# Softmax sums applied after the value product: one division for two heads, the sums spread by DMAs through DRAM

## The chip, the cores and the metric

The kernel runs on one core of a Trainium2 chip. The metric is the device time of one launch in microseconds (us). The time before is the median of three runs; next to it stands one profiled execution, from which every duration below is taken.

## The reference, cut to what matters

The program is a small decoder trunk on one sequence of 512 tokens with 1024 channels: one state-space layer with its MLP, a shared projection for keys, values and forget gates, one layer of forgetting attention with its MLP, and a final norm. All of it is float32. The change lies in the attention alone, 16 heads of 64 channels:

```python
def one_block(args):                       # one block of 128 queries
    s = jnp.einsum('bhqd,bhkd->bhqk', qb, k)
    s = s + fq[..., None] - cum_log_f[:, :, None, :]
    s = jnp.where(mask[None, None], s, -jnp.inf)
    p = jax.nn.softmax(s, axis=-1)         # exp(s - max) / sum
    return jnp.einsum('bhqk,bhkd->bhqd', p, v)
```

Dividing each row of exponentials by its sum before the product with v, or dividing the row of the product by that sum afterwards, gives the same result.

## The kernel before, in words

Matrix products are made from float32 values split into a high and a low part (float32r), with three passes per product; ScalarE (ACT) copies the high part out and VectorE (DVE) subtracts to get the low part. Large weights come in 512 KB loads `st` (line 113), are split by ACT (line 124) into `wt`, and the low part of these splits is made in the attention by GpSimd (POOL, line 128).

The attention is a list of 64 steps, `steps`: head 0 to 15, and in each head four query blocks `i` of 128 rows; block `i` sees `i+1` blocks of 128 keys. It is a schedule written out by hand (`manual_schedule`, line 1411): each engine, and SyncE's queue of DMAs (SP), issues its instructions in the order in which the loop over `n` emits them. In one turn of this loop the letters of `CFG["seq"]` are called in order, `s f o q l a n t p x` for even `n` and `s o f l n t a p x q` for odd `n`:

- `s` makes the logits of step n on TensorE (PE) (`st_s`, lines 1210 to 1212, into `psx`), the row maximum on DVE and the exponential on ACT with the row sum accumulated beside it (`st_x`, lines 1218 and 1220). Where `i` is 3 it also issues five DMAs on SP that bring the next but one head's keys and queries (`st_h`, line 1203).
- `n` divides the exponentials of step n: a reciprocal of 128x1 and a multiplication of 128 rows by 128 to 512 columns on DVE (`st_n`, lines 1225 and 1229).
- `t` transposes the exponentials of step n-1 on PE (`st_t`, line 1234, into `ptp`), `p` copies them out as high and low part (`st_p`, ACT line 1249, DVE line 1250).
- `a`, at odd `n`, multiplies two blocks with the values (`st_av`, line 1268, into `po`). The left operand holds the values' high and low part side by side, so that `po` has 128 partitions for one head.
- `q` and `o` take a finished head out (`st_o`): ACT copies the lower half of `po` into `of` (line 1275), one turn later DVE adds the upper half (line 1277). Two heads share one `of` of 128x512; after the second head ACT copies it to `ot` (line 1281), and a turn later DVE makes the low part (line 1283).
- `f` puts one piece of other matrix work on PE into the turn: the key and value projections of later heads (lines 810 and 1130), later the first half of the output projection (`pw`, line 810). At every fourth turn such a piece opens a new weight chunk, and then ACT splits the next `st`. `l` runs deferred work: POOL's low part, and behind it on SP the next load `st`, which waits for POOL; and DVE's additions (line 1334) and low parts.

So DVE, ACT and SP each have one order, and a wait of one instruction holds all that stand behind it there. Instructions written after the loop (the preparation of the next MLP's first weights from `sr`, lines 887 to 899) are placed in between by the program's planner. Temporary tiles `tmp` rotate over four buffers.

After the loop the last head is taken out, and the second half of the output projection (`po`, line 810) and the next MLP follow.

Of the kernel before, what the change touches and what calls it, by code (L numbers as in the profile page):

```python
# [9 lines left out]
F32 = mybir.dt.float32  # L10
F32R = mybir.dt.float32r
I32 = mybir.dt.int32
AF = mybir.ActivationFunctionType
ALU = mybir.AluOpType
AX = mybir.AxisListType
PSUM = bass.MemoryType.PSUM

P = 128
SEQ = 512
# [10 lines left out]
NH = 16  # L30
HD = 64
EPS = 1e-6
MAGIC = 12582912.0
TWO_PI = 2.0 * math.pi
CFG = dict(seq=['sfoqlantpx', 'soflntapxq'], pat=[2, 1, 1, 1, 1, 1, 1, 1, 1, 1, 1, 1, 1, 1, 1, 1, 1, 1, 1, 1, 1, 1, 1, 1, 1, 1, 1, 1, 1, 1, 1, 1, 1, 1, 0, 2, 1, 1, 1, 1, 1, 1, 1, 1, 1, 1, 1, 1, 1, 1, 1, 1, 1, 1, 1, 1, 1, 1, 1, 1, 1, 1, 2, 1, 1, 1], nl=4, nt=1, u0=66, ns=[], wk=4, st=['f u02 u03 u10 u11 u12 s u13 c0 c1', 't t u02 f t u03 u10 u11 t u12 u13 s c0 c1'], x='GGGGGGGGGGVbb', m0=3)
WQ = "AABBABABAB"
ORDER = """
LR mR kz gnl win2V_0 win1V_0 decS_0 dl_1 rxv wina_0 gl_1 sw_2_0 gn win2V_1 xsS_1_1 dl_0 gR sw_2_1 xsS_0_1 tk
# [19 lines left out]
def body(tc, x, mix_norm, mlp_norm, mlp_w1, mlp_w2, log_dt, a_re, a_im, b_re, b_im,  # L58
         c_re, c_im, ssm_d, w_glu, kv_norm, w_kvf, b_f, wq, wo, final_norm, out):
    nc = tc.nc  # L60
    V, S, G, TE, DMA = nc.vector, nc.scalar, nc.gpsimd, nc.tensor, nc.sync

    with ExitStack() as ctx:
# [14 lines left out]
        def act_t(name):  # L78
            return ap_.tile([P, 2, SEQ], F32R, name=name, tag="act")

        def pst(name):
            return ps.tile([P, 512], F32, name=name, tag="ps")

        ident = cp.tile([P, P], F32, name="ident")
# [666 lines left out]
        hp = ctx.enter_context(tc.tile_pool(name="hp", bufs=1))  # L751
        m2 = ctx.enter_context(tc.tile_pool(name="m2", bufs=2))
        kvp = ctx.enter_context(tc.tile_pool(name="kvp", bufs=1))

        def act2_t(name):
            return m2.tile([P, 2, SEQ], F32R, name=name, tag="act2", bufs=8)

        def tmp_t(name, bufs=4):
            return m2.tile([P, SEQ], F32, name=name, tag="tmp", bufs=bufs)
# [235 lines left out]
        for mp in range(KT // 2):  # L995
            if mp == CFG["m0"]:
                u0 = Mix(mlp_w1_[0], 0, H, arena)
                run(u0.prep())
            for n in (2 * mp, 2 * mp + 1):
                c0 = n % 2 * D + n // 2 * 256  # L1000
# [77 lines left out]
        for m in range(KT):  # L1078
            h = act_t("hq")
# [6 lines left out]
        for k0 in (0, 3, 6):  # L1086
            nk_ = min(3, KT - k0)
            st = stp.tile([P, 4, 256], F32, name="st", tag="st").rearrange("p k n -> p (k n)")[:, 0:nk_ * VF]
            st = st.rearrange("p (k n) -> p k n", n=VF)
# [115 lines left out]
        def st_s(hd, i):  # L1205
            X = HX[hd % 2]
            n = P * (i + 1)
            qs = slice(i * P, (i + 1) * P)
            psx = pst("psx")
            TE.matmul(psx[:, 0:n], QT[hd // 2][:, hd % 2, qs], X[:, 0, 0:n], start=True, stop=False)  # L1210
            TE.matmul(psx[:, 0:n], X[0:66, 1, qs], X[0:66, 2, 0:n], start=False, stop=False)
            TE.matmul(psx[:, i * P:n], identr, mneg_r, start=False, stop=True)
            return psx

        def st_x(psx, i):
            n = P * (i + 1)
            mx = m2.tile([P, 3], F32, name="mx", tag="mx", bufs=6)
            V.tensor_reduce(mx[:, 0:1], psx[:, 0:n], AX.X, ALU.max, negate=True)  # L1218
            pb_ = m2.tile([P, SEQ], F32, name="prob", tag="prob", bufs=2)
            S.activation(pb_[:, 0:n], psx[:, 0:n], AF.Exp, bias=mx[:, 0:1], accum_out=mx[:, 1:2])  # L1220
            return pb_, mx

        def st_n(pb_, mx, i):
            n = P * (i + 1)
            V.reciprocal(mx[:, 2:3], mx[:, 1:2])
            if i in CFG["ns"]:
                S.activation(pb_[:, 0:n], pb_[:, 0:n], AF.Copy, scale=mx[:, 2:3])
            else:
                V.tensor_scalar(pb_[:, 0:n], pb_[:, 0:n], mx[:, 2:3], None, ALU.mult)  # L1229

        def st_t(pb_, i):
            ptp = pst("ptp")
            for kt in range(i + 1):
                TE.transpose(ptp[:, kt * P:(kt + 1) * P], pb_[:, kt * P:(kt + 1) * P], ident)  # L1234
            return ptp
# [36 lines left out]
        def st_o(hd):  # L1272
            po, of = head["po"], head["of"]
            rs = slice((hd % 2) * 64, (hd % 2) * 64 + 64)
            S.activation(of[rs], po[64:128], AF.Copy)
            yield
            V.tensor_tensor(of[rs], po[0:64], of[rs], op=ALU.add)
            if hd % 2:
                ot = act_t("ot")
                OT.append(ot)  # L1280
                S.activation(ot[:, 0], of, AF.Copy)
                yield
                V.tensor_tensor(ot[:, 1], of, ot[:, 0].bitcast(F32), op=ALU.subtract)
# [53 lines left out]
        NST = len(steps)  # L1337
# [15 lines left out]
        def at_s(n):  # L1353
            if n == CFG["u0"]:
                u0.arena = make_arena()
            if CFG["u0"] <= 60 and n in (CFG["u0"], 60):
                later.extend([lambda: next(u0p, 0)] * (8 if n < 60 else 3))
            if n < NST:
                ex[n] = st_x(st_s(*steps[n]), steps[n][1])
                hd, i = steps[n]  # L1360
                if i == 3 and hd + 2 < NH:
                    st_h(hd + 2)
# [19 lines left out]

        def at_t(n):
            if 0 <= n - 1 < NST:
                tp[0] = st_t(ex[n - 1][0], steps[n - 1][1])

        def at_n(n):
            if n < NST:
                st_n(*ex[n], steps[n][1])

        def at_p(n):
            if 0 <= n - 1 < NST:
# [176 lines left out]
```

## Time and profile before

| | |
|---|---|
| median of 3 runs | 1200.35 us (1198.94 to 1211.31) |
| profiled execution, its own time | 1199.35 us |
| span of this execution, first to last instruction | 1197.6 us |
| PE matmul busy | 1119.2 us, 93% of the span |
| DVE busy | 912.1 us, 76% |
| ACT busy | 607.8 us, 51% |
| POOL busy | 291.2 us, 24% |
| mean granted TensorE clock | 0.972 of full speed |

The profile lists for each engine how long it was busy; a group of instructions is named by line, engine, operation and tile. Idle time stands with the work that ended it ("releaser"). The time outside the span is 1.75 us. The attention's 64 steps run from about 636 to 813 us.

### The profile page before, as it was taken

How to read it: one execution, taken by the hardware profiler on the slowest of the kernel's cores; microseconds unless marked ns; L12 is line 12 of the kernel's file. 1: busy time of each engine (PE TensorE's matmuls, PEld its weight loads, DVE VectorE, ACT ScalarE, POOL GpSimd, SP SyncE). 2: the span in 40 equal slices, each digit the busy share in tenths (PEclk: the TensorE clock that was granted, in tenths of full speed). 3: DMA queues.
4: the chain of work that ended last, by engine and by line, in shares of the span. 5: the costliest groups of instructions: out<-in, count | busy, mean ns of one | idle time of the engine just before them, and what ended most of it. 6: DMA issues, size and time to landing. Idle time of an engine off the chain costs nothing.

```text
span 1197.6 us, 19030 instructions
## 1 busy us (share of the span) xinstructions
PE 1119.2 (93%) x7189; PEld 996.8 (83%) x7189; DVE 912.1 (76%) x1639; ACT 607.8 (51%) x1106; POOL 291.2 (24%) x298
## 2 busy tenths in 40 slices
PE   1678899999999999999999999888899999999997
PEld 1567688899999898998888999776899898999986
DVE  8976548799877778768566878875999777778754
ACT  4985355454434444336345666554755444343433
POOL 4234214422121212203102222314322312213101
PEclk9878899999999999999999999989899999999999
DMA  7997753143322323233244444311143323233222
GB/s 165 218 183 151 176 165 106 42 143 99 122 90 90 107 86 124 88 103 117 65 132 133 107 107 133 98 54 53 35 128 104 111 82 124 88 117 96 89 88 71
DMA packets 109388, 131.37 MB, mean 110 GB/s; under 512 B 9360, under 2 KB 87984, under 8 KB 109296
## 3 DMA queue, kind: packets, MB, share of 16 engines
q1 hardware_dynamic: 104432, 117.57, 32.9%
q0 software_dynamic: 4864, 12.59, 6.1%
q8 instruction: 57, 0.93, 0.3%
q14 instruction: 35, 0.29, 0.1%
HBM read 103.21 MB, written 2.74 MB: 88 GB/s over the span
## 4 chain that ended last, share of the span: by engine, by line
PE 79%; DVE 8%; DMA 5%; ACT 3%; issue 3%; SPq 0%; POOL 0%; DVEq 0%; ACTq 0%; POOLq 0%
PE pu L919 25%; PE po L810 16%; PE pvs L1484 14%; PE pk L810 6%; PE pv L810 6%; PE pvs L1130 2%; PE po L1268 2%; DMA cc<-dt 1%; PE ptp L1234 1%; PE pf L1118 1%; DMA TW<-tB 1%; DVE prob L1229 1%; DMA bc<-in_ssm_b_im_dram 1%; DMA TW<-kd 1%; PE pv L731 1%
## 5 line engine op out<-in xcount | busy, mean ns | idle before, releaser
L919 PE MATMUL pu<-hm,ar 128*128 128x256 f32 x1536 | 228.9, 284 | 3.2 <-ACT hm L863 2.2
L919 PEld LDWEIGHTS pu<-hm,ar 128*128 128x128 f32 x1536 | 204.4, 193 | 4.5 <-ACT hm L863 2.6
L810 PE MATMUL po<-at,wt 128*128 128x512 f32 x768 | 176.9, 389 | 0.0
L1484 PE MATMUL pvs<-wt,at 128*128 128x512 f32 (+1 forms) x768 | 175.5, 388 | 0.0
L898 POOL TENSOR_TENSOR ar<-ar,st 128x256 f32<-128x256 f32 x62 | 71.8, 1160 | 423.1 <-DVE ar L894 404.3
L124 ACT ACTIVATE wt<-st 128x1024 fp32r<-128x1024 f32 x110 | 116.2, 1057 | 114.0 <-PE po L810 30.3
L810 PEld LDWEIGHTS po<-at,wt 128*128 128x128 f32 x768 | 143.2, 188 | 29.1
L1484 PEld LDWEIGHTS pvs<-wt,at 128*128 128x128 f32 x768 | 142.6, 188 | 28.8
L128 DVE TENSOR_TENSOR wt<-st,wt 128x1024 fp32r<-128x1024 f32 x90 | 117.1, 1302 | 27.9 <-ACT wt L124 27.7
L919 PE MATMUL pu<-hd,x 128*128 128x256 f32 x768 | 136.3, 285 | 0.0
L887 ACT ACTIVATE ar<-ar 128x512 fp32r<-128x512 f32 x128 | 77.0, 627 | 89.9 <-PE pu L919 83.7
L919 PEld LDWEIGHTS pu<-hd,x 128*128 128x128 f32 x768 | 113.4, 193 | 2.9 <-issue 0.5
L888 DVE TENSOR_TENSOR ar<-ar 128x512 fp32r<-128x512 f32 x128 | 88.8, 700 | 31.0 <-ACT ar L887 31.0
L887 ACT ACTIVATE x<-st 128x512 fp32r<-128x512 f32 x62 | 36.3, 625 | 99.8 <-PE pvs L1484 48.9
L128 POOL TENSOR_TENSOR wt<-st,wt 128x1024 fp32r<-128x1024 f32 x20 | 48.2, 2408 | 143.6 <-ACT wt L124 125.5
L894 DVE TENSOR_TENSOR ar<-st 128x512 f32<-128x512 f32 x62 | 50.6, 819 | 32.8 <-DMA st<-in_mlp_w_dram 32.1
L810 PE MATMUL pv<-zt,wt 128*128 128x512 f32 x312 | 72.4, 391 | 0.2 <-ACT hT L992 0.2
L810 PEld LDWEIGHTS pv<-zt,wt 128*128 128x128 f32 x312 | 58.2, 188 | 12.3 <-ACT hT L992 0.4
L1220 ACT ACTIVATE prob<-psx,mx 128x128 f32<-128x128 f32 (+1 forms) x64 | 33.8, 528 | 60.2 <-DVE mx L1218 60.2
L899 POOL TENSOR_TENSOR ar<-ar,st 128x256 f32<-128x256 f32 x62 | 60.4, 977 | 4.2
L1039 ACT ACTIVATE at<-c 128x512 fp32r<-128x512 f32 x64 | 39.7, 630 | 39.3 <-DVE c L1037 39.1
L1025 DVE TENSOR_TENSOR hT<-hT,po 128x512 f32<-128x512 f32 x64 | 43.4, 679 | 16.8 <-PE po L810 16.8
(333 smaller groups left out, 2046.2 us busy)
## 6 DMA issues: line engine op xcount, KB each, us to landing
st<-in_mlp_w_dram SPq DMA_DIRECT2D x126, 512.0 KB
st<-in_ssm_w_glu_dram SPq DMA_DIRECT2D x16, 512.0 KB
st<-in_w_kvf_dram SPq DMA_DIRECT2D x14, 512.0 KB
hx<-kt SPq DMA_DIRECT2D x48, 128.0 KB
Win<-tB POOLq DMA_DIRECT2D x8, 512.0 KB, 7.3
TW<-tB POOLq DMA_DIRECT2D x8, 512.0 KB, 6.3
TW<-kd SPq DMA_DIRECT2D x8, 512.0 KB
st<-in_attn_wq_dram SPq DMA_DIRECT2D x8, 512.0 KB
```

The source lines that it names most:

```text
L124: S.activation(wt[:, 0], st, AF.Copy)
L128: (G if slot[1] == "A" and CFG["x"][7 + lows[0] % 3] == "G" else V).tensor_tensor(wt[:, 1], st, wt[:, 0].bitcast(F32), op=ALU.subtract)
L810: TE.matmul(pts[m], wt[:, a, k, m * P:(m + 1) * P], acts[k0 + k][:, b], start=(first and k0 == parts[0][0] and k == 0 and n == 0), stop=(k ...
L887: S.activation(X[0], src, AF.Copy)
L888: V.tensor_tensor(X[1], src, X[0].bitcast(F32), op=ALU.subtract)
L894: V.tensor_tensor(Ta[:, :, js].rearrange("p w j n -> p j w n"), f[:, :, 1:3], f[:, :, 0:1].broadcast_to([P, 2, 2, P]), op=ALU.add)
L898: e.tensor_tensor(Tb[:, 0, js], Ta[:, 0, js], v[:, :, 1, 0], op=ALU.add)
L899: e.tensor_tensor(Tb[:, 1, js], Tb[:, 0, js], v[:, :, 1, 1], op=ALU.add)
L919: TE.matmul(self.acc[p], self.W[p][:, a, j], self.H.moving(p, j, b), start=(p == g[0] and j == 0 and n == 0), stop=(p == g[-1] and j == 3 ...
L1025: V.tensor_tensor(hT[:, m, :], hT[:, m, :], po[j], op=ALU.add)
L1039: S.activation(at_[:, 0], c, AF.Square)
L1484: TE.matmul(po[:, cols], A[k][:, b], wts[k // 2][:, a, k % 2, cols], start=start and n == 0, stop=stop and n == 3 * len(ks) - 1)
```

## The change

The exponentials are no longer multiplied by the reciprocal of their sum. The sums of two heads go into one tile `sums` of 128x8 (a column for each head and block). One turn after the pair's last step (`n`, `st_r`) DVE takes the reciprocal of all eight columns, and SP writes them to DRAM transposed, as 8 rows of 128. One turn later (`st_d`) SP reads them back in two DMAs, each with one head's row of 512 repeated over 64 partitions, into `rb` (128x512). When the pair is taken out, `of` is multiplied by `rb` on DVE, one turn after the addition; the copy to `ot` and its low part follow after that. The last pair does without DRAM: eight small matmuls with the reciprocals as left operand and the identity as right operand spread them into a tile of PSUM, and the multiplication follows the addition directly.

```diff
+        dq = ctx.enter_context(tc.tile_pool(name="dq", bufs=1, space=bass.MemoryType.DRAM))
...
-        def st_x(psx, i):
+        SUMS, RECS = {}, {}
+
+        def st_x(psx, hd, i):
             n = P * (i + 1)
-            mx = m2.tile([P, 3], F32, name="mx", tag="mx", bufs=6)
-            V.tensor_reduce(mx[:, 0:1], psx[:, 0:n], AX.X, ALU.max, negate=True)
+            if i == 0 and hd % 2 == 0:
+                SUMS[hd // 2] = m2.tile([P, 8], F32, name="sums", tag="sums", bufs=2)
+            c = hd % 2 * 4 + i
+            mx = m2.tile([P, 1], F32, name="mx", tag="mx", bufs=4)
+            V.tensor_reduce(mx, psx[:, 0:n], AX.X, ALU.max, negate=True)
             pb_ = m2.tile([P, SEQ], F32, name="prob", tag="prob", bufs=2)
-            S.activation(pb_[:, 0:n], psx[:, 0:n], AF.Exp, bias=mx[:, 0:1], accum_out=mx[:, 1:2])
-            return pb_, mx
-
-        def st_n(pb_, mx, i):
-            n = P * (i + 1)
-            V.reciprocal(mx[:, 2:3], mx[:, 1:2])
-            if i in CFG["ns"]:
-                S.activation(pb_[:, 0:n], pb_[:, 0:n], AF.Copy, scale=mx[:, 2:3])
+            S.activation(pb_[:, 0:n], psx[:, 0:n], AF.Exp, bias=mx, accum_out=SUMS[hd // 2][:, c:c + 1])
+            return pb_
+
+        RB = {}
+        rd = [dq.tile([8, P], F32, name=f"rd{i}", tag=f"rd{i}", bufs=1) for i in range(2)]
+
+        def st_r(pr):
+            sm = SUMS.pop(pr)
+            V.reciprocal(sm, sm)
+            if pr == NH // 2 - 1:
+                RECS[pr] = sm
             else:
-                V.tensor_scalar(pb_[:, 0:n], pb_[:, 0:n], mx[:, 2:3], None, ALU.mult)
+                DMA.dma_start(rd[pr % 2].rearrange("c q -> q c"), sm)
+
+        def st_d(pr):
+            if pr < NH // 2 - 1:
+                RB[pr] = tmp_t("rb")
+                v = rd[pr % 2][0:1, 0:1]
+                for h in range(2):
+                    DMA.dma_start(RB[pr][h * HD:(h + 1) * HD],
+                                  bass.AP(tensor=v.tensor, offset=v.offset + h * SEQ, ap=[[0, HD], [1, SEQ]]))
+
+        def st_b(pr):
+            rh = RECS.pop(pr)
+            rb = pst("rb")
+            for i in range(4):
+                for h in range(2):
+                    c = h * 4 + i
+                    TE.matmul(rb[h * HD:(h + 1) * HD, i * P:(i + 1) * P], rh[:, c:c + 1].broadcast_to([P, HD]), ident,
+                              start=i == 0, stop=i == 3)
+            return rb
...
             S.activation(of[rs], po[64:128], AF.Copy)
+            pr = hd // 2
+            last = pr == NH // 2 - 1
+            if hd % 2 and last:
+                RB[pr] = st_b(pr)
             yield
             V.tensor_tensor(of[rs], po[0:64], of[rs], op=ALU.add)
             if hd % 2:
+                if not last:
+                    yield
+                V.tensor_tensor(of, of, RB.pop(pr), op=ALU.mult)
                 ot = act_t("ot")
                 OT.append(ot)
                 S.activation(ot[:, 0], of, AF.Copy)
...
         def at_n(n):
-            if n < NST:
-                st_n(*ex[n], steps[n][1])
+            if 0 <= n - 1 < NST and steps[n - 1][0] % 2 and steps[n - 1][1] == 3:
+                st_r(steps[n - 1][0] // 2)
+            if 0 <= n - 2 < NST and steps[n - 2][0] % 2 and steps[n - 2][1] == 3:
+                st_d(steps[n - 2][0] // 2)
```

## Rows read from the trace of the kernel before

**Rows 1.** Windows: span, us, busy PE, PEld, DVE, ACT, POOL; clock, DMA share, GB/s.
```profile
660.00:740.00 80.00, 79.70 (x563) 73.46 (x562) 64.46 (x157) 51.15 (x129) 19.13 (x8) 1.00 0.40 107
740.00:813.00 73.00, 60.98 (x364) 53.21 (x362) 60.75 (x128) 39.37 (x97) 17.87 (x10) 0.93 0.30 87
813.00:825.00 12.00, 12.00 (x53) 9.85 (x51) 2.76 (x4) 1.82 (x3) 1.48 (x2) 0.86 0.15 44
```

**Rows 2.** Groups of DVE instructions, 637 to 825 us: busy us, mean ns | idle before.
```profile
L1229 DVE TENSOR_SCALAR prob<-prob,mx 128x128 f32<-128x128 f32 (+1 forms) x64 | 33.1, 517 | 2.2
...
L1225 DVE RECIPROCAL mx<-mx 128x1 f32<-128x1 f32 x64 | 10.3, 161 | 18.8 <-ACT prob L1220 17.3
```

**Rows 3.** Waits, 637 to 825 us: us in total, times, longest us.
```profile
PE ptp L1234 <- DVE prob L1229: 12.7, 8, 3.0
```

**Rows 4.** Timeline of the late steps: start us, us, instruction [idle before, releaser].
```profile
784.58 2.37 POOL L128 TENSOR_TENSOR wt<-st,wt 128x1024 fp32r<-128x1024 f32 x1 [9.23 <-ACT wt L124]
784.64 2.59 DVE L1229 TENSOR_SCALAR prob<-prob,mx 128x512 f32<-128x512 f32 x1
...
787.37 0.63 PE L1234 MATMUL ptp<-ident,prob 128*128 128x128 f32 x4 [1.61 <-DVE prob L1229]
...
796.21 3.44 DVE L888 TENSOR_TENSOR x<-sr,x 128x512 fp32r<-128x512 f32 x2
...
800.39 1.09 PE L1234 MATMUL ptp<-ident,prob 128*128 128x128 f32 x4 [3.03 <-DVE prob L1229]
```

**Rows 5.** Timeline: weight loads on SP, and DVE's first instruction of turn m+4.
```profile
659.91 0.37 SPq L113 DMA_DIRECT2D st<-in_w_kvf_dram  x1
...
666.24 0.68 DVE L1283 TENSOR_TENSOR ot<-of,ot 128x512 fp32r<-128x512 f32 x1
...
680.34 0.37 SPq L113 DMA_DIRECT2D st<-in_w_kvf_dram  x1
...
685.94 0.68 DVE L1283 TENSOR_TENSOR ot<-of,ot 128x512 fp32r<-128x512 f32 x1
...
786.97 0.37 SPq L113 DMA_DIRECT2D st<-in_attn_wo_dram  x1
...
794.41 0.68 DVE L1283 TENSOR_TENSOR ot<-of,ot 128x512 fp32r<-128x512 f32 x1
```

**Rows 6.** Timeline, turns 18 to 21: ACT's order, and the next transpose's weight load.
```profile
684.07 0.63 ACT L1281 ACTIVATE ot<-of 128x512 fp32r<-128x512 f32 x1
...
686.74 1.05 ACT L124 ACTIVATE wt<-st 128x1024 fp32r<-128x1024 f32 x1
...
689.25 0.19 ACT L1220 ACTIVATION_READ_ACCUMULATOR prob<-psx,mx 128x1 f32 x1
...
690.62 0.14 PEld L1234 LDWEIGHTS ptp<-ident,prob 128*128 128x128 f32 x1
```

**Rows 7.** Timeline: DMAs on SP, and the instruction that waited for each.
```profile
24.34 0.29 SPq L259 DMA_DIRECT2D gl<-in_mlp_norm_dram  x1
...
25.85 0.28 PE L705 MATMUL pg<-ident,gl 32*128 32x32 f32 x1 [1.35 <-DMA gl<-in_mlp_norm_dram]
...
82.30 0.31 SPq L607 DMA_DIRECT2D kd<-ks  x1
88.25 0.58 SPq L613 DMA_DIRECT2D TW<-kd  x1
...
98.20 0.31 SPq L607 DMA_DIRECT2D kd<-ks  x1
101.05 0.58 SPq L613 DMA_DIRECT2D TW<-kd  x1
...
535.05 0.94 SPq L1092 DMA_DIRECT2D st<-in_w_kvf_dram  x1
...
538.22 0.75 ACT L1095 ACTIVATE w<-st 128x272 fp32r<-128x272 f32 x2 [1.17 <-DMA st<-in_w_kvf_dram]
```

More of the change, by code (lines that the diff above doesn't have):

```diff
@@ L34 @@
 TWO_PI = 2.0 * math.pi
-CFG = dict(seq=['sfoqlantpx', 'soflntapxq'], pat=[2, 1, 1, 1, 1, 1, 1, 1, 1, 1, 1, 1, 1, 1, 1, 1, 1, 1, 1, 1, 1, 1, 1, 1, 1, 1, 1, 1, 1, 1, 1, 1, 1, 1, 0, 2, 1, 1, 1, 1, 1, 1, 1, 1, 1, 1, 1, 1, 1, 1, 1, 1, 1, 1, 1, 1, 1, 1, 1, 1, 1, 1, 2, 1, 1, 1], nl=4, nt=1, u0=66, ns=[], wk=4, st=['f u02 u03 u10 u11 u12 s u13 c0 c1', 't t u02 f t u03 u10 u11 t u12 u13 s c0 c1'], x='GGGGGGGGGGVbb', m0=3)
+CFG = dict(seq=['sfoqlantpx', 'soflntapxq'], pat=[2, 1, 1, 1, 1, 1, 1, 1, 1, 1, 1, 1, 1, 1, 1, 1, 1, 1, 1, 1, 1, 1, 1, 1, 1, 1, 1, 1, 1, 1, 1, 1, 1, 1, 0, 2, 1, 1, 1, 1, 1, 1, 1, 1, 1, 1, 1, 1, 1, 1, 1, 1, 1, 1, 1, 1, 1, 1, 1, 1, 1, 1, 2, 1, 1, 1], nl=4, nt=1, u0=66, wk=4, st=['f u02 u03 u10 u11 u12 s u13 c0 c1', 't t u02 f t u03 u10 u11 t u12 u13 s c0 c1'], x='GGGGGGGGGGVbb', m0=3)
 WQ = "AABBABABAB"
@@ L1358, in at_s @@
             if n < NST:
-                ex[n] = st_x(st_s(*steps[n]), steps[n][1])
+                ex[n] = st_x(st_s(*steps[n]), *steps[n])
                 hd, i = steps[n]
@@ L1384, in at_t @@
             if 0 <= n - 1 < NST:
-                tp[0] = st_t(ex[n - 1][0], steps[n - 1][1])
+                tp[0] = st_t(ex[n - 1], steps[n - 1][1])
         def at_n(n):
-            if n < NST:
-                st_n(*ex[n], steps[n][1])
+            if 0 <= n - 1 < NST and steps[n - 1][0] % 2 and steps[n - 1][1] == 3:
+                st_r(steps[n - 1][0] // 2)
+            if 0 <= n - 2 < NST and steps[n - 2][0] % 2 and steps[n - 2][1] == 3:
+                st_d(steps[n - 2][0] // 2)
         def at_p(n):
```

## The prediction, made before the changed kernel was run

> **What bounds the kernel now.** I read the busy shares of the whole span first, and they mislead here: PE is busy 93% of it, so I went to windows of the attention. Two stretches differ. From 660 to 740 us PE is busy 79.70 of 80 us at the full clock [rows 1]: whatever is taken from DVE there is worth nothing, since PE's own list of products is the bound. From 740 to 813 us PE is busy only 60.98 of 73 us, so it idles 12.0 us, while DVE is busy 60.75, and the granted clock falls to 0.93 of full, and to 0.86 in the 12 us behind [rows 1]. There DVE is the limit. The table of waits names the work: the transposes waited eight times, 12.7 us in all, for the division of the exponentials [rows 3]. The timeline shows why they are long: the multiplication of 128x512, begun just after POOL's subtraction, took 2.59 us and ended with it, and PE idled 1.61 us; another gap of 3.03 us came from 3.44 us of other DVE work that stood before the division, and after it four transposes took 1.09 us where they take 0.63, so PE ran at about half its clock [rows 4].
>
> **What goes.** 64 multiplications (33.1 us) and 64 reciprocals (10.3 us) leave DVE, 43.4 us [rows 2]. Eight reciprocals of about 0.16 us and eight multiplications of 128x512 come back; the nearest row is the subtraction of the same shape at 0.68 us [rows 5], so 8 x 0.84 = 6.7 us. The net of 36.7 us is spread over the whole attention, and only what falls behind 740 us can move the end, at most the 12.0 us of idle time [rows 1, 3]. Not all of it: after the change a transpose waits for the exponential alone, but the exponential waits for the maximum, which stands on DVE behind the same other work. The gap of 1.61 us closes (the division itself was late), of the one of 3.03 us I expect PE to gain the one product group ahead that it may now run. I take half, 6 us. The clock's bound is 0.07 x 73 + 0.14 x 12 = 6.8 us; since the clock fell behind the long gaps, which shrink, I take 2 us of it. Gain: 8 us, with ends 0 and 12.0 + 6.8 = 18.8.
>
> **What comes: a round trip through DRAM.** Call m the last step of a pair. SP's order in turns m to m+2 is: five head DMAs, the weight load (which waits for POOL), then the write of the sums, then the two reads. The reciprocal itself needs sums that are ready by then. So the write is issued when the weight load's issue ends. The product with `rb` stands on DVE behind the maximum in turn m+4, where the kernel before has the subtraction for `ot`. From the end of the load's issue to there it is 5.96 us for the first of the seven pairs, 5.23 for the second, 7.07 for the last [rows 5]; I take 5.8 for all.
>
> How long the trip takes, no row shows, since nothing of before writes single elements of 4 bytes. The write moves 1024 of them. Bounds: the kernel before writes 64 KB to DRAM and reads it back in the same way; from the write's issue to that of its reader it took 2.85 us at best and 5.95 in a longer clean pair [rows 7]. A load of 384 pieces of 64 bytes, issued right behind a load of 384 KB on the same queue, had landed 3.17 us after its issue [rows 7]. The write here stands behind 512 KB and has more pieces, so I take 4.2 us, above that row and in the middle of the bounds; ends 2.85 and 5.95. The two reads are issued in 0.58 us each, 1.16 together. The landing after the issue took 1.22 us for 4 KB (25.85 less 24.34 and 0.29) and 2.23 us for the small pieces (538.22 less 535.05 and 0.94) [rows 7]; 128 KB each is nearer to the second, 2.2 us. Sum: 4.2 + 1.16 + 2.2 = 7.6 us, against 5.8: the product waits 1.8 us. With the ends, 2.85 + 1.16 + 1.22 = 5.2 (in time) and 5.95 + 1.16 + 2.2 = 9.3 (3.5 us late).
>
> The Trainium skill (DMA: Bandwidth & Descriptors, Anatomy of one DMA) gives a transfer about 2.0 us plus its bytes at 436 GB/s; estimated from that page the write takes 2.0 us and the last read 2.3, and by it the spread sums would come in time. The same page (Specifications; Rules for kernel authors) says against this change that a strided last dimension becomes one descriptor for each element, and that pieces under 512 bytes cost a read and a write back; no run here shows either, and it gives no time for them.
>
> **Who waits behind it.** The waiting product holds on DVE the low part of the last exponentials, the next maximum and all that follows. On ACT it holds the copy to `ot` (0.63 us), and behind that in the same order the weight split (1.05 us), the copy of the transposes and the next exponential [rows 6]. Before, the split began at 686.74, and the exponential's accumulator was read at 689.44, while PE came to the transposes that need it at 690.62: 1.18 us of slack [rows 6]. With the product in time the split begins at 685.94 + 0.68 + 0.63 = 687.25, 0.5 us later. So 0.7 us of lateness is hidden, and the rest reaches PE: 1.8 - 0.7 = 1.1 us, seven times, 7.7 or about 8 us. This falls on pairs in the PE-bound stretch as well as in the late one. POOL's subtraction stands behind the split, so it is pushed back too and can't meet the waiting product.
>
> SP waits for the write's landing before it reads; behind it are the head DMAs of turn m+4, due a whole head later, and the weight loads, with three chunks ahead: both hidden; if that cover is gone, PE's pieces wait for weights. `rb` takes a buffer of `tmp`; in the rotation each comes free several turns earlier: nothing. Eight matmuls more are under 1 us on PE.
>
> **The tail.** The last pair gets one multiplication more (0.68 us) and its small matmuls ahead of `ot`, on the way to the output projection; other products lie beside it, I take 1 us (ends 0 and 2).
>
> **Sum.** -8 + 8 + 1 = +1 us on the profiled execution's 1199.35 us (span 1197.6 and 1.75 around it), which is 1 us under the median of the runs; on the median that is 1201 us. A change of under about 1% (12 us) can't be told from none here.
>
> **Rivals.**
> *The sums land in time.* Write 2.85, reads 1.16 and 1.22: 5.2 us against 5.8, no stall; the gain stands alone. With the gaps closed as I sized them, -8 + 1 gives 1193; with most of the gaps (10) and clock (5) 1186. For it: the best rows above, and DMAs at 0.40 of their capacity in this stretch [rows 1]. Against: 512 KB just ahead on the queue. Chance 0.18 for under 1188.
>
> *The write of single elements is slow, and the stall takes the clock with it.* At 5.95 us the product is 3.5 us late, 2.8 us reach PE, seven times: 20 us. Gaps of that size are where the clock fell before (3.03 us fell, 1.61 did not [rows 4]); about 2 us more each, 14 us. Sum -8 + 20 + 14 + 1 = +27, 1227 us; with the clock held 1213. It decides from a trip of about 8.6 us on, where PE's gap passes 2 us. For it: 1024 pieces, the write to DRAM, and no cover on ACT. Chance 0.34 for over 1212.
>
> *It gives DVE time, but the bound isn't DVE's sum of work.* The gaps are then only moved to the other DVE work in front of the maximum, gain 2 and stall 2: within 1% as well.
>
> **How the numbers follow.** The wash, with the third rival, has 0.48: faster by over 1% 0.18, within 1% 0.48, slower 0.34. The predicted time is the wash's, 1201 us; its own range is 1190 to 1212. The range over the cases runs from the full gain, 1186, to the slow write, 1226.
>
> **What would show it.** Lines 1225 and 1229 gone, and waits of the transposes for DVE with them. New waits of DVE for a DMA on `rb`, seven, of 1 to 3 us each; SP waiting for the write about 4 us; the gaps of PE one turn behind, in the stretch that had none. PE idle from 740 to 813 at about half. Wrong would be: no wait on `rb` at all (then faster), waits above 3 us with the clock under 1.00 before 740 us (then slower), or transposes that wait for the exponential as long as they did for the division.

## The result: 6.5% slower, and the profile after

The changed kernel takes 1284.19 us (median of four runs, 1275.49 to 1286.27) against 1202.79 for the kernel before, run beside it: a ratio of 1.0652, 95% interval 1.0609 to 1.0694. The prediction was 1201 us, its range ended at 1226, and slower by over 1% had a chance of 0.34. The profiled execution has a span of 1284.5 us against 1197.6.

The divisions of the exponentials are gone, and with them the transposes' waits for DVE [rows 3]. In their place the table of waits of the changed kernel, 630 to 920 us, shows (us in total, times, longest):

```profile
ACT ot L1315 <- DVE of L1312: 69.5, 8, 11.8
DVE of L1312 <- DMA rb<-rd: 66.0, 7, 11.6
PEld ptp L1261 <- ACT prob L1226: 53.5, 7, 12.0
...
PE ptp L1261 <- ACT prob L1226: 51.4, 6, 11.8
...
DVE ar L895 <- DMA sr<-in_mlp_w_dram: 11.7, 1, 11.7
```

Read it as one chain: the multiplication by the spread sums (line 1312) waits for its DMA, ACT's copy waits for the multiplication, the exponential stands behind that copy, and PE's transposes wait for the exponential. In the fifth pair the spread sums cost DVE only 0.18 us of wait, because it had already waited 11.7 us for a load of the next MLP's weights (`sr`), issued 2.5 us behind the write; experiments 10 to 14 come back to that load. One pair out of seven on the timeline (start us, us, instruction, idle before and its releaser), the rows that answer to [rows 5, 6]:

```profile
700.52 1.60 PE L811 MATMUL pk<-hk,wt 128*128 128x512 f32 x6
701.03 0.37 SPq L113 DMA_DIRECT2D st<-in_w_kvf_dram  x1
701.50 0.46 SPq L1238 DMA_DIRECT2D rd<-sums  x1
...
712.24 1.12 SPq L1245 DMA_DIRECT2D rb<-rd  x2
...
717.26 0.69 DVE L1312 TENSOR_TENSOR of<-of,rb 128x512 f32<-128x512 f32 x1 [10.56 <-DMA rb<-rd]
717.99 0.63 ACT L1315 ACTIVATE ot<-of 128x512 fp32r<-128x512 f32 x1 [10.41 <-DVE of L1312]
...
721.33 0.48 PE L1261 MATMUL ptp<-ident,prob 128*128 128x128 f32 x1 [9.45 <-ACT prob L1226]
...
725.59 2.07 PE L811 MATMUL pk<-hk,wt 128*128 128x512 f32 x6
```

The write (line 1238) is issued at 701.50, and the reads that wait for it at 712.24: 10.74 us. In the seven pairs this was 10.7 to 13.3 us. From the first read to the multiplication another 5.02 us pass, so the trip takes 15.8 us where DVE was free after 5.3 (706.70 less 701.40, the end of the load's issue). PE idles 9.45 us, and behind the gap six products take 2.07 us that took 1.60 before it. The same windows as [rows 1], of the changed kernel (span, us, busy PE, PEld, DVE, ACT, POOL, clock, DMA share, GB/s):

```profile
660.00:740.00 80.00, 59.50 (x384) 54.06 (x383) 36.96 (x67) 33.68 (x84) 11.87 (x5) 0.85 0.32 74
740.00:813.00 73.00, 50.96 (x322) 45.79 (x320) 27.24 (x50) 26.13 (x66) 9.48 (x4) 0.81 0.30 68
813.00:825.00 12.00, 0.78 (x2) 0.47 (x2) 4.88 (x6) 3.62 (x8) 4.12 (x3) 0.60 0.56 140
```

The stretch that had no gap is now idle a quarter of the time, at a clock of 0.85. To set the runs side by side I use one measure, the **loop**: from the first product of the first logits (`psx`) to the last transpose (`ptp`) of the attention. The next three fences are its one window in the kernel before, in the changed one, and in the changed one without its DMAs (experiment 3 below):

```profile
635.40:812.60 177.20, 163.72 (x1062) 146.41 (x1060) 142.91 (x323) 105.44 (x259) 44.16 (x21) 0.97 0.37 99
```

```profile
644.00:901.10 257.10, 180.98 (x1061) 159.03 (x1061) 114.06 (x208) 105.53 (x259) 43.65 (x21) 0.82 0.32 76
```

```profile
637.50:809.30 171.80, 162.56 (x1062) 146.13 (x1060) 113.94 (x208) 104.70 (x259) 44.30 (x21) 0.98 0.38 103
```

Same products of PE (1061 or 1062) in all three. The loop grew by 79.9 us, about the loss by the medians (81.4 us). The profiled span grew by 86.9 us, but 8.6 us of that lie before the loop, in work that the change leaves as it was and that took 635 to 649 us in the profiled executions; so the loop, of one profiled execution each, tells more than the span. Against the version without DMAs it is 85.3 us longer: 66.9 us more idle time of PE (76.1 less 9.2) and 18.4 us more busy time for the same products, which is the lower clock.

### The profile page after: what moved, and what is told of

The parts are those of the page before. It is cut to its first block, busy times and chain, and to the rows that moved or that the text cites. A ratio compares the mean times of both kernels' runs of the same rounds, so it can differ in the third digit from the quotient of the medians.

```text
span 1284.5 us, 19027 instructions
## 1 busy us (share of the span) xinstructions
PE 1142.7 (89%) x7205; PEld 1012.7 (79%) x7205; DVE 882.0 (69%) x1527; ACT 610.4 (48%) x1106; POOL 299.0 (23%) x298
## 2 busy tenths in 40 slices
DMA packets 117787, 133.23 MB, mean 104 GB/s; under 512 B 16864, under 2 KB 95488, under 8 KB 117696
## 5 line engine op out<-in xcount | busy, mean ns | idle before, releaser
L899 POOL TENSOR_TENSOR ar<-ar,st 128x256 f32<-128x256 f32 x62 | 80.1, 1294 | 417.2 <-DVE ar L895 386.5
L1261 PE MATMUL ptp<-ident,prob 128*128 128x128 f32 x160 | 29.8, 284 | 51.4 <-ACT prob L1226 51.4
L895 DVE TENSOR_TENSOR ar<-st 128x512 f32<-128x512 f32 x62 | 50.1, 812 | 29.6 <-DMA st<-in_mlp_w_dram 28.7
L1261 PEld LDWEIGHTS ptp<-ident,prob 128*128 128x128 f32 x160 | 20.7, 145 | 57.5 <-ACT prob L1226 53.5
L900 POOL TENSOR_TENSOR ar<-ar,st 128x256 f32<-128x256 f32 x62 | 58.3, 943 | 4.2
```

Source lines behind the costliest of these rows:

```text
L895: V.tensor_tensor(Ta[:, :, js].rearrange("p w j n -> p j w n"), f[:, :, 1:3], f[:, :, 0:1].broadcast_to([P, 2, 2, P]), op=ALU.add)
L899: e.tensor_tensor(Tb[:, 0, js], Ta[:, 0, js], v[:, :, 1, 0], op=ALU.add)
L900: e.tensor_tensor(Tb[:, 1, js], Tb[:, 0, js], v[:, :, 1, 1], op=ALU.add)
```

## The experiments

Ratios are to the kernel before, run beside each kernel; times in us are the ratio times the median of the kernel before that ran beside it (1203.6 to 1205.3).

**1 and 2. Fewer pieces in the write.**

```diff
-rd = [dq.tile([8, P], F32, ...)]          # both: 2 buffers
+rd = [dq.tile([P, 8], F32, ...)]
-DMA.dma_start(rd[pr % 2].rearrange("c q -> q c"), sm)
+DMA.dma_start(rd[pr % 2], sm)
```

> The pair's sums are written to DRAM as they lie, 128 rows of 32 B, in place of 1024 single elements of 4 B; both reads are unchanged, so the sums come back in another order and the rows of the output are scaled by the wrong sums. Same bytes, same queue, same number of transfers and waits. Theory (the number of pieces sets the write's time, 10.7 to 12.1 us at 1024 pieces): the write takes about 3 us, the trip about 8, the multiplication waits 2 us or less per pair, the time is 1200 to 1215 us. Rival (the write stands behind the weight loads of 512 KB on the same DMA engines, or waits for DRAM's answer, whatever its pieces): the write still takes about 11 us and the time stays at 1275 to 1290 us.

```diff
-DMA.dma_start(rd[pr % 2].rearrange("c q -> q c"), sm)
+DMA.dma_start(rd[pr % 2][0:4].rearrange("c q -> q c"), sm[:, 0:4])
...
-offset=v.offset + h * SEQ
+offset=v.offset
```

> Only the first four of the eight columns are written, element by element (512 pieces of 4 B); both reads take the first head's row, so the second head of each pair is scaled by the first head's sums. Theory (time per piece on the 16 engines): the write falls by about half, to 6 to 6.5 us, the trip from 16 to about 11, the wait per pair from 10.6 to 5 to 6 us, the time to about 1235 us (1225 to 1250). Rival (a fixed cost of any write that starts here): the write stays at about 11 us, the time at 1275 to 1290 us.

Rows of 32 B: ratio 1.0117 (1.0031 to 1.0203), about 1218 us. The write is 3.0 to 3.7 us long, and the table of waits of this run, 630 to 910 us, is that of the changed kernel with a sixth of the time in its first row:

```profile
DVE of L1312 <- DMA rb<-rd: 11.0, 7, 2.2
...
PE po L1295 <- DVE pB L1277: 8.0, 8, 1.6
PE ptp L1261 <- ACT prob L1226: 6.2, 8, 1.4
```

So the form of the write makes most of the loss; a load of 512 KB stood just ahead of it here too. What is left of it, 14 us, is not the late sums alone. The table's second row here is another gap of PE, one in every pair. In the second pair:

```profile
700.15 1.90 DVE L1317 TENSOR_TENSOR ot<-of,ot 128x512 fp32r<-128x512 f32 x1
...
700.84 0.33 PE L1261 MATMUL ptp<-ident,prob 128*128 128x128 f32 x1 [0.87 <-ACT prob L1226]
...
701.98 0.68 DVE L1277 TENSOR_TENSOR pB<-ptp,pB 128x512 fp32r<-128x512 f32 x1
...
702.71 1.04 PE L1295 MATMUL po<-pB,vt 128*128 128x256 f32 x7 [1.00 <-DVE pB L1277]
...
704.17 2.87 PE L811 MATMUL pk<-hk,wt 128*128 128x512 f32 x6
```

The low part of `ot` (line 1317) takes 1.90 us here, the low part of the exponentials (line 1277) stands behind it on DVE, and PE waits 1.00 us for that. Why it takes 1.90 us is told under experiments 10 to 14. Behind the two gaps six products take 2.87 us, at a granted clock of 0.50 of full. Half the elements: ratio 1.0553 (1.0483 to 1.0623), 1270 us. The write still took 8.8 to 11.1 us and the multiplication waited 55.9 us in all. My expectation that the time goes with the number of pieces was wrong, and so was the rival of a fixed cost, since rows of 32 B are fast. That needed experiment 5.

**3 and 4. No DMAs, and DMAs that nobody on DVE waits for.**

```diff
-DMA.dma_start(rd[pr % 2].rearrange("c q -> q c"), sm)     # experiment 3 only
+pass
-if pr < NH // 2 - 1:        # in st_d; experiment 3 only
+if pr < 0:
...
-V.tensor_tensor(of, of, RB.pop(pr), op=ALU.mult)          # 3 and 4, all but the last pair
+V.tensor_tensor(ofv, ofv, ones.unsqueeze(1).broadcast_to([P, 4, P]), op=ALU.mult)
```

> No write and no reads; the multiplication of the first seven pairs takes a tile of ones that is in SBUF already, so the outputs of 14 heads are not divided. What is left of the change is the work that VectorE lost: two scalings of the probabilities per step for one multiplication per pair. Theory (the forecast's gain term of 8 us was right and the trip alone made the loss): 1193 us (1185 to 1198), stage 187 us in place of 195. Rival (VectorE's work never bound the stage): 1199 to 1203 us. Second rival (the loss is of the multiplication or of the output's chain through ScalarE and not of the DMAs): above 1215 us.

> All writes and reads are issued as in the changed kernel, but the multiplication of the first seven pairs takes a tile of ones, so nothing on VectorE waits for what the reads bring; 14 heads are not divided. Theory (VectorE's wait for the spread sums makes the loss): within 3 us of the kernel without the transfers, about 1193 to 1198 us. Rival (SyncE, held for 11 us by the reads' wait for the write, brings the next loads of hidden states and weights late): 1210 us or more, with SyncE's wait for the write still 11 us per pair and idle time of TensorE that ends on one of those loads.

Without DMAs 0.9986 (0.9956 to 1.0017); with unread DMAs 1.0010 (0.9979 to 1.0041), SP still waiting 69.9 us for the seven writes. So DVE's wait makes the loss, and SP's wait for the writes costs at most a few us of it (the two loops are 171.8 and 176.2 us). But the gain that I had put at 8 us was not in the time: the first rival of experiment 3 holds, at first sight. The loop of experiment 3 did get 5.4 us shorter (171.8 against 177.2), which raised the question that experiments 10 to 14 answer.

**5 and 6. The write by itself.** Each pair writes in another form; the wait of the element read back is the write's time.

```diff
+DMA.dma_start(d.rearrange("c q -> q c"), sm[:, 0:k])    # k rows of 128, element by element
+DMA.dma_start(d[:, :, 0], sm)    # d is [P, 8, w]: elements 4 w bytes apart
+DMA.dma_start(d, sm)             # 128 rows of 32 B
...
+DMA.dma_start(RB[pr][0:1, 0:1], rd[pr][0:1, 0:1])       # SP waits for the write here
```

> A measurement of the write by itself: as in the run whose spread sums are not used (the multiplication of the first seven pairs takes ones, 14 heads are not divided), but each of the seven pairs writes its reciprocals in another form, and SyncE then reads one element back, so its wait is the write's time. Forms in the order of the pairs: 8 rows of 128, element by element as in the change (1024 pieces of 4 B, 128 to each stretch of 512 B); 1024 pieces, each in a stretch of 512 B of its own; 1024 pieces 64 B apart (8 to a stretch); 256 pieces in two rows of 128; 128 rows of 32 B; 1024 pieces 8 B apart (64 to a stretch); 128 pieces in one row. Measured so far: 1024 pieces 10.7 to 12.1 us, 512 pieces 8.8 to 11.1, 128 rows of 32 B 3.2 to 3.7. Theory A (pieces share the engines; time goes by their number): 11, 11, 11, 5, 3.2, 11, 3 us. Theory B (pieces that fall into the same 512 B follow one another at about 70 ns): 11, 3, 3 to 4, 9, 3.2, 6, 9 us.

> The write by itself again, in other forms and another order (the multiplication takes ones, 14 heads are not divided; SyncE reads one element back). Forms: 128 rows of 32 B; 128 pieces of 4 B in one row of 512 B; 128 pieces in eight groups of 16 neighbours (64 B), each group in a stretch of 512 B of its own; 1024 pieces, each in a stretch of its own; 128 pieces, each in a stretch of its own; 1024 pieces 8 B apart; 8 rows of 128 element by element, as in the change. Measured before, once each: 3.0, 7.7, not measured, 4.0, not measured, 7.15, 9.4 us. Theory (small pieces that fall into the same 512 B follow one another): 3.0, 7.7, 3 to 4.5, 4.0, about 3, 7, 9.4 to 11 us. Rival (they follow one another within 64 B): the same, but 7 to 8 us for the third. Rival (the order of the pairs or the traffic beside them made the differences): the times go with the pair's place and not with the form.

SP's timeline in the second of these runs (each write and the read that waited for it):

```profile
684.15 0.45 SPq L1243 DMA_DIRECT2D rd<-sums  x1
691.99 0.25 SPq L1255 DMA_DIRECT2D rb<-rd  x1
704.74 0.65 SPq L1246 DMA_DIRECT2D rd<-sums  x1
708.40 0.25 SPq L1255 DMA_DIRECT2D rb<-rd  x1
725.45 0.58 SPq L1250 DMA_DIRECT2D rd<-sums  x1
729.15 0.25 SPq L1255 DMA_DIRECT2D rb<-rd  x1
...
794.27 0.44 SPq L1243 DMA_DIRECT2D rd<-sums  x1
804.47 0.26 SPq L1255 DMA_DIRECT2D rb<-rd  x1
```

They are: 128 elements that make one row of 512 B (7.84 us), 128 elements in eight groups of 16 neighbours (3.66), 1024 elements each in 512 B of its own (3.70), and the change's form (10.20). All forms:

| form | pieces | pieces in one stretch of 512 B | us, run 5 | us, run 6 |
|---|---|---|---|---|
| 4 B, each alone in 512 B | 128 | 1 | | 2.97 |
| rows of 32 B | 128 | 16 | 2.97 | 3.15 |
| 4 B, groups of 16 neighbours | 128 | 16 | | 3.66 |
| 4 B, each alone in 512 B | 1024 | 1 | 4.00 | 3.70 |
| 4 B, 64 B apart | 1024 | 8 | 4.65 | |
| 4 B, 8 B apart | 1024 | 64 | 7.15 | 7.02 |
| 4 B, one row | 128 | 128 | 7.73 | 7.84 |
| 4 B, two rows | 256 | 128 | 7.80 | |
| 4 B, eight rows (the change) | 1024 | 128 | 9.43 | 10.20 |

Eight times as many pieces cost about 1 us where each has its own 512 B. Putting 128 of them into one stretch of 512 B costs nearly 5 us even when there are no others. The groups of 16 neighbours, as dense as the full row but in eight stretches, are fast, so the dense 64 B alone don't do it. How the pieces of a write are shared out over the 16 DMA engines was not seen, and the groups are written as 8 by 16 where the full row is 128 by 1; whether pieces that one engine writes into a stretch, or pieces of several engines, hold each other up stays open. The order of the pairs was another in the two runs, and the forms that stand in both agree within 0.8 us. The theory of experiment 5 that counts the pieces in a stretch (B) holds in its order, not in its slope: 64 in a stretch cost nearly as much as 128.

**7 to 9. The wait moved.** The multiplication stands later; `of` moves into a larger buffer for that.

```diff
-                    head["of"] = tmp_t("of")
+                    head["of"] = ap_.tile([P, 2, SEQ], F32, name="of", tag="act")[:, 0]
...
-                if not last:
+                for _ in range(0 if last else k):     # k = 7: six turns later (7); 3: two (8); 6: five (9)
                     yield
...
-if 0 <= n - 2 < NST and ...: st_d(...)                # experiment 7 only
+if 0 <= n - 7 < NST and ...: st_d(...)
```

> Nothing is left out: the same write and the same two reads, but the reads are issued at turn m+7 in place of m+2 and the multiplication by the spread sums stands six turns later (the output stays in a larger buffer meanwhile). Theory (the trip of 16 us and the wait for it are the whole loss; the work taken from VectorE is worth about 1 us, as without the transfers): no wait for the spread sums, 1198 to 1206 us. Rival (the slow write or the later chain to the output projection costs in itself): above 1212 us, with a new wait of TensorE for the outputs, or of ScalarE for the multiplication.

> Nothing is left out; the write and the reads stand where the change has them, only the multiplication by the spread sums stands two turns later (a turn of this stretch is 2.75 us, so 5.5 us). Theory (what is late of the trip, less a slack of about 0.7 us on ScalarE, reaches TensorE, and the low clock behind each gap adds to it): the wait falls from 66.0/7 = 9.4 to about 4 us per pair, TensorE's gap to about 3.3; 7 x 3.3 plus 7 x 2 to 3 us for the clock is 37 to 44 us over the late multiplication's run, 1238 to 1246 us. Rival (the multiplication's place matters for what stands behind it, not for the wait): no proportion, 1215 or less, or 1265 or more.

> Nothing is left out; the write and the reads stand where the change has them, only the multiplication stands five turns later (13.8 us). Theory (only VectorE's wait costs, SyncE's wait for the write is hidden): no wait for the spread sums, 1198 to 1207 us, while SyncE still waits 10 to 12 us for each write. Rival (SyncE's wait delays the next loads): 1212 us or more.

Six turns later: 0.9979 (0.9948 to 1.0011), 1203 us, no wait for the spread sums. The whole trip stays, its loss is gone. Two turns later: 1.0195 (1.0142 to 1.0248), 1228 us, a wait of 22.6 us in all, PE idle 19.6 us in the loop. That is under the 1238 to 1246 expected, because the wait left was 3.2 us per pair and not 4, and because the late run to which the theory adds has 11.8 us of idle time of its own; but the loss follows the wait as the theory has it. Five turns later with the reads in their old place: 1.0054 (1.0026 to 1.0083), 1211 us, above the theory's range. There is no wait for the sums, but one gap of PE of 11.3 us:

```profile
749.35 0.37 SPq L1238 DMA_DIRECT2D rd<-sums  x1
...
758.94 1.12 SPq L1245 DMA_DIRECT2D rb<-rd  x2
760.15 1.81 SPq L1384 DMA_DIRECT2D sr<-in_mlp_w_dram  x2
...
765.91 0.69 DVE L895 TENSOR_TENSOR ar<-sr 128x512 f32<-128x512 f32 x1 [10.71 <-DMA sr<-in_mlp_w_dram]
...
771.83 0.48 PE L1261 MATMUL ptp<-ident,prob 128*128 128x128 f32 x1 [11.30 <-ACT prob L1226]
```

Here the rival is right once in the loop: the two loads of the next MLP's weights stand behind the reads, which wait for the write, and so are issued 10.8 us after it. In the version of six turns later the same loads are issued 2.5 us behind the write, yet PE idles 7.3 and 3.1 us for them; experiments 10 to 14 follow that.

**The sums spread by PE**, for every pair as for the last one:

```diff
-if hd % 2 and last:
+if hd % 2:
     RB[pr] = st_b(pr)
```

> Nothing is left out, and no DRAM: each pair's sums are spread over the partitions by 16 small matmuls on TensorE, as the changed kernel does for the last pair, and the multiplication follows the addition at once. The 16 took 1.98 us for the last pair of the run without transfers. Theory (TensorE bounds the stage, so these matmuls add to it: 7 x 1.0 to 2.0 us, less the 1 us that VectorE's relief is worth): 1208 to 1216 us. Rival (they find room in the gaps that TensorE had, 12 us of 73 in the late stretch): 1198 to 1205 us.

1.0030 (0.9998 to 1.0062), 1209 us: the theory's figure. PE is busy 169.8 us in the loop where the version without DMAs has 162.6; the 128 small products (each of a pair's eight stands twice in the trace) take 9.6 us, 1.2 us per pair.

**PE kept busy in the gaps.**

```diff
 ptp = pst("ptp")
+for _ in range(nfill):       # 80 in the step behind a multiplication
+    TE.transpose(ptp[:, 0:P], ident, ident)
```

> The changed kernel, with 80 transposes of the identity (128x128, result overwritten) added on TensorE ahead of the transposes that wait behind each multiplication, so that TensorE works through most of the 9.4 us in which it idles. Theory (beside the gaps, the granted clock costs: half of full for some 6 us behind each gap, 7 x 3 us): the clock stays at 1.00 from 660 to 740 us, the time falls by 14 to 21 us, to 1263 to 1270 us, although work was added. Rival (the clock costs nothing beside the gaps): 1284 us or more.

1.0682 (1.0629 to 1.0736): no gain, the theory's number missed. The added work as a group (busy us, mean ns, idle before) and the loop's window:

```profile
L1261 PE MATMUL ptp<-ident 128*128 128x128 f32 x560 | 67.2, 285 | 10.7 <-DVE vt L1144 10.7
```

```profile
636.00:893.10 257.10, 228.44 (x1622) 211.02 (x1620) 113.58 (x208) 105.62 (x259) 43.79 (x21) 0.95 0.31 76
```

The kernel's own products took 228.4 less 67.2 = 161.2 us, as at full clock, against 181.0 in the changed kernel: the slow products are the clock's doing. But the filling took as long as the gaps, two of the fills themselves waited for DVE (10.7 us), and of the rest of the 28.7 us of idle time I can't say which part the filling made. So that the clock's 18.4 us come off the time when the gaps stay is not shown.

**10 to 14. Where the gain was.** The late version with no DMA (10), with the write two turns later (11), with the write issued by GpSimd (12); and then two full versions (13, 14).

```diff
-DMA.dma_start(rd[pr % 2].rearrange("c q -> q c"), sm)
+pass                                                        # 10 (multiplication by ones)
+G.dma_start(rd[pr % 2].rearrange("c q -> q c"), sm)         # 12
...
+if 0 <= n - 3 < NST - 1 and ...: DMA.dma_start(...)         # 11, the write at turn m+3
```

> No write and no reads, the multiplication (by ones for the first seven pairs, 14 heads not divided) six turns later, as in the late version. The control for the two runs beside it: what the attention costs with VectorE relieved and no DMA added. Theory (in the late version two loads of the next MLP's weights landed 11 to 13 us after their issue behind the write of single elements, against 3.7 to 5.2 before, and TensorE idled 7.3 + 3.1 us for them; that gap hides the gain): without the write the gap is 3 to 4 us, the loop of the attention takes 163 to 168 us in place of 172.7, the time is 1190 to 1197 us. Rival (the burst of preparation work on VectorE makes the gap, whatever lands): loop 171 to 173 us, time 1199 to 1204 us.

> Nothing is left out. The late version with the write two turns later still (turn m+3), behind the MLP's two loads on SyncE instead of ahead of them. Theory (the write holds up what is issued behind it on its queue): these loads land 4 to 5 us after their issue, no idle time of TensorE above 5 us, loop 164 to 169 us, time 1191 to 1198 us, about 0.7% under the kernel before. Rival (the gap is not the write's doing): loop 172 to 174, time 1200 to 1204 us.

> Nothing is left out. The late version with the write issued by GpSimd on its own queue, at the same turn. Theory A (loads wait behind the write because they share a queue): as with the later write, the MLP's loads land in 4 to 6 us, time 1191 to 1198 us. Theory B (they share the 16 engines, whatever the queue): they still take 10 us or more, time 1200 to 1204 us. Either way GpSimd pays for the issue of 1024 pieces; where that is several us, its low parts and the loads behind them come later.

Without DMAs 0.9931 (0.9904 to 0.9958), a gain of 8.3 us, loop 166.1: the forecast's gain is there. The later write 0.9988 (0.9968 to 1.0009) and the write by GpSimd 0.9986 (0.9961 to 1.0011), loops 173.9 and 173.2. The later write tested nothing: in the compiled order the two loads of the MLP moved back as well and stood 2.5 us behind the write again. The timeline of the version with GpSimd's write shows the meeting:

```profile
745.37 0.90 POOL L1238 DMA_DIRECT2D rd<-sums  x1 [0.96 <-DVE sums L1234]
747.62 0.92 SPq L1384 DMA_DIRECT2D sr<-in_mlp_w_dram  x2
759.22 0.69 DVE L895 TENSOR_TENSOR ar<-sr 128x512 f32<-128x512 f32 x1 [8.68 <-DMA sr<-in_mlp_w_dram]
...
763.64 0.47 PE L1261 MATMUL ptp<-ident,prob 128*128 128x128 f32 x1 [7.95 <-ACT prob L1226]
```

The load is used 11.6 us after its issue (759.22 less 747.62), though the write was on another queue; in the late versions with SP's write it was 10.9 and 11.3 us, and in the kernel before and in the one without DMAs 3.7 us. DVE and ACT wait for it, and PE idles 7.95 us once. So theory A is out: the queue doesn't matter. That the 16 engines are what the write and the load share, as theory B has it, fits; the run can't tell them from something else that both use. The Trainium skill (DMA: Bandwidth & Descriptors, Issuing engines are not separate DMA queues) says that DMAs run on the same 16 engines whichever engine started them; the run agrees, with 11.6 us against 10.9.

```diff
+def st_w(pr):                                # 13, at turn m+2
+    pt = pst("pt")
+    TE.transpose(pt[0:8, 0:P], RECS.pop(pr), ident)
+    row = head["full"][0:8, 1, 0:P]
+    S.activation(row, pt[0:8, 0:P], AF.Copy)
+    DMA.dma_start(rd[pr % 2], row)           # 8 rows of 512 B
...
-if pr == NH // 2 - 1:                        # 14: st_r, st_d, st_o
+if pr in (4, NH // 2 - 1):
```

> Nothing is left out. TensorE transposes the 128x8 reciprocals of a pair, ScalarE copies the 8x128 out, and SyncE writes 8 rows of 512 B to DRAM in place of 1024 single elements; reads at turn m+7, multiplication six turns later, as in the late version. Theory (the single elements hold up the 16 engines, and with that the MLP's loads; without them the gain of the control shows): the MLP's loads land 4 to 6 us after their issue, loop 165 to 169 us, 1194 to 1199 us, 0.4 to 0.8% under the kernel before. Rival (the reads of 2 x 128 KB delay them too, or the extra steps on TensorE and ScalarE cost a microsecond a pair): 1201 to 1206 us.

> Nothing is left out. The late version in which the fifth pair alone, whose write met the MLP's two loads, is spread by TensorE as the last one is, without DRAM; six pairs are still written element by element. Theory (only this meeting cost): no idle time of TensorE above 5 us, loop 165 to 170 us, 1194 to 1199 us. Rival (the other six writes cost as well, in ways spread over the loop): 1200 to 1204 us.

0.9916 (0.9882 to 0.9949) with rows of 512 B, and 0.9927 (0.9902 to 0.9951) with the fifth pair's sums spread by PE: both about 0.8% under the kernel before, loops 166.6 us in both. The load that met the write, in the version with rows of 512 B:

```profile
743.20 0.30 SPq L1243 DMA_DIRECT2D rd<-of  x1
743.60 0.92 SPq L1390 DMA_DIRECT2D sr<-in_mlp_w_dram  x2
...
747.26 0.69 DVE L895 TENSOR_TENSOR ar<-sr 128x512 f32<-128x512 f32 x1 [0.77 <-DMA sr<-in_mlp_w_dram]
```

It is used 3.7 us after its issue, right behind a write. In the other version six slow writes remain and cost nothing that can be measured. So the change does pay, by 0.8%, once the write is in rows or meets no load that is needed soon, and the multiplication stands late enough.

One difference is left: without DMAs the loop is 171.8 us with the multiplication where the change has it (171 to 172 in the two runs on the write's form, where nothing waits for a DMA either), and 166.1 six turns later. The group of the low part of `ot` tells it; experiment 3 first, then experiment 10 (busy us, mean ns):

```profile
L1321 DVE TENSOR_TENSOR ot<-of,ot 128x512 fp32r<-128x512 f32 x8 | 13.3, 1669 | 0.7 <-ACT ot L1319 0.7
```

```profile
L1321 DVE TENSOR_TENSOR ot<-of,ot 128x512 fp32r<-128x512 f32 x8 | 5.5, 683 | 0.7 <-ACT ot L1319 0.7
```

On the timeline of experiment 3 this subtraction runs beside POOL's low part of the weights and ends with it:

```profile
709.85 2.39 POOL L128 TENSOR_TENSOR wt<-st,wt 128x1024 fp32r<-128x1024 f32 x1 [8.36 <-ACT wt L124]
710.86 1.93 DVE L1321 TENSOR_TENSOR ot<-of,ot 128x512 fp32r<-128x512 f32 x1
```

Started 1.01 us after POOL's instruction, it lasts until that one's end (712.24) and its own 0.55 us more. The place that the change gave the subtraction meets POOL in six of the seven pairs, 7.8 us of DVE in all. It reaches PE: in experiment 3 each of the six is followed by a gap of PE of 0.27 to 1.04 us that ends on the low part `pB` (line 1277), the next on DVE, and experiment 10 has no such collision and no such gap. They are 3.4 us together, part of this row of experiment 3's waits:

```profile
PE po L1295 <- DVE pB L1277: 7.5, 7, 4.1
```

So the collision is the likely cause of most of the 5.7 us; no run took it away alone. The Trainium skill (SBUF — State Buffer, Who interferes with whom) says that a DVE instruction with two inputs in SBUF contends with a GpSimd instruction that reads SBUF. The rows agree: 1.93 us against 0.68.

## Why the prediction was wrong, step by step

- **The write's time, 4.2 us with ends of 2.85 and 5.95: the step that failed.** It measured 10.7 to 13.3 us, and 9.4 and 10.2 by itself. I bounded a transfer of 1024 elements by rows of wide pieces [rows 7], took the dearest of them as the upper end, and let the number of pieces count a little. What the runs put in its place is less the bytes or the number of pieces than how many small pieces fall into the same 512 B: the transposed layout puts 128 there. No row of before could show it, and an upper end taken from transfers without that property bounded nothing. The profile's packets under 512 B rose from 9360 to 16864, that is 7504 more, near 7 x 1024 = 7168; with rows of 32 B there were 10592, and the difference of 6272 is 7 x (1024 - 128), one packet for each piece. The Trainium skill (DMA: Bandwidth & Descriptors, Specifications; Rules for kernel authors), as cited in the prediction, has a descriptor for each element of a strided last dimension, and a read and a write back for pieces under 512 B; the packets agree with the first, and the dearer writes into a shared stretch speak for the second. I had left it without weight since no row priced it. The other estimate in the prediction, 2.0 us for the write by the Trainium skill (DMA: Bandwidth & Descriptors, Anatomy of one DMA), is further off than my own; that fit is of DMAs issued by GpSimd, and here SP issues.
- **The window of 5.8 us before DVE needs the sums**: 5.3 us in the pair shown, 4.7 to 5.7 in six of the seven. Nearly right.
- **The reads, 1.16 + 2.2 us**: 4.8 to 5.0 us in the first two pairs, 3.6 to 5.9 in all; short by about 1.3 us.
- **What is late less a cover of 0.7 us reaches PE.** Right in mechanism: 10.56 us of wait gave 9.45 us of idle PE, and with rows of 32 B waits of 1.50 to 2.23 us in the first four pairs gave 0.26 to 0.87, so the cover was 1.1 to 1.4 us and not 0.7. That run is nearly the case I forecast (trip 6.8 to 7.4 us, late 1.5 to 2.2), and it was 14 us slower; I had +1 for it. The difference is the missing gain, the clock (both below) and a second path that I had not counted: the low part of `ot`, slowed beside POOL, delays the next low part on DVE; PE waited 8.0 us in all for that one, and 6.2 us for the exponentials.
- **The clock** stood as a cost only in the slow-write rival, at 2 us per gap. The changed kernel lost 18.4 / 7 = 2.6 us per pair, and the run with rows of 32 B had its PE busy 10.6 us longer (173.2 against 162.6) with gaps of only about 1 us, two in each pair. I had taken gaps under 1.6 us as free of it, from a single one [rows 4].
- **The gain of 8 us**: 8.3 us without DMAs and with a late multiplication, so the sum of DVE's work did bound the late stretch. That 8 was met so closely is in part luck, since I had taken half of a bound: in the loop PE's idle time fell by 8.5 us (13.5 to 5.0) and its busy time by 2.6. At the change's own place it was 1.7 us and not to be told from none: I wrote that POOL's subtraction can't meet the waiting product, and looked no further; it meets the subtraction that follows.
- **SP's wait hidden**: right for the head DMAs and the weight loads that I had counted. I had not counted the next MLP's two loads, once in the loop: in experiment 9 they stood behind SP's wait, and in the other late versions they ran beside the write and were used 7 to 8 us later.
- **The rival with the slow write** had the right mechanism, and its point of decision (a trip of 8.6 us) was passed by far. With the measured sizes its sum would have been 7 x (15.8 - 5.3 - 0.7) = 69 for the gaps, 18 for the clock, 5 off for the loop's gain and 1 for the tail: +83, against a measured +78 (0.0652 x 1202.79); the terms are read from the same runs, so this checks the path and forecasts nothing. Its price came from the same wrong upper end, and the range with it.

## What to carry to other kernels

Count, for a DMA that turns a tile around, how many elements land in the same 512 B: with 64 or more of them the writes here took 7.0 to 13.3 us, with 16 or fewer 3.0 to 4.7. Let TensorE do the turn so that whole rows are written; that kernel was 0.8% under the one before, though its write was not timed by itself. Put the consumer of any trip through DRAM where a wrong estimate of it is covered several times over, since in a schedule with fixed orders the wait runs through all engines, and behind the gaps PE worked at the lower clock (18.4 us more busy time beside 66.9 us more idle time). When relieving an engine seems to bring nothing, test the relief alone in more than one place of the order: here the gain existed; in one place one late load hid it, in the other probably a collision with POOL.

## What the runs showed of the hardware that was not expected

- A write of 512 B as 128 elements (7.7 and 7.8 us) takes twice as long as one of 4 KB as 1024 elements spread over 512 KB (3.7 and 4.0 us). Whether the stretch is exactly 512 B was not tried: 16 neighbours in 64 B are fast when alone in their 512 B, 64 elements in 512 B are slow.
- While such a write runs, a load of 512 KB that takes 3.7 us is used 10.9 to 11.6 us after its issue, whichever engine's queue issued the write.
- Two gaps of PE of about 1 us or less, close together, were followed by a lower granted clock. In experiment 1 PE idled 0.87 and 1.00 us between 699.97 and 702.71 us, and from 704 to 706 us the clock was 0.50 of full, which is 1.2 GHz; by 708 us it was 1.00 again, 2.4 GHz. It fell so in six of the seven pairs; in the seventh, with 0.47 and 1.02 us, it did not. Over the loop it was 0.94, and 0.98 in experiment 3.
